# Small tiles in pools of their own: a decoder layer whose matmul pages are moved within SBUF

## The chip, the cores and the metric

The kernel runs on one core of a Trainium2 chip. The metric is the device time of one execution in microseconds; several executions give a median. A separate execution is taken with the hardware profiler, and all rows below are from that one.

## What is computed

One layer of a hybrid decoder, for 512 tokens of width 1024, in float32. Four sub-layers follow each other, each closed by a layer norm of (alpha x + f(x)):

```python
x = layer_norm(DN_ALPHA * x + 0.5 * swiglu_ffn(x, ffn1_wg, ffn1_wu, ffn1_wd), ln1_g, ln1_b)   # d_ff 2816
y = parallel_mixers(x, w_in, ...)          # gated DeltaNet with 8 heads beside a convolution module
x = layer_norm(DN_ALPHA * x + y, ln2_g, ln2_b)
x = layer_norm(DN_ALPHA * x + memory_cross_attention(x, mem, w_xq, w_xkv, w_xo), ln3_g, ln3_b)  # 256 memory tokens
x = layer_norm(DN_ALPHA * x + 0.5 * swiglu_ffn(x, ffn2_wg, ffn2_wu, ffn2_wd), ln4_g, ln4_b)

def swiglu_ffn(x, w_gate, w_up, w_down):
    return (silu(x @ w_gate) * (x @ w_up)) @ w_down
```

The mixers project the stream, run a short convolution and a chunked delta rule per head, gate and normalise its output, run a convolution of width 31 with a channel norm, project both branches, mix them with two gates and project again.

## The kernel before

**Split products.** A float32 matrix product is made of three products of a reduced-precision type. Each operand is split into an upper part (ScalarE's copy, line 267) and a lower part (VectorE's subtraction, line 268); upper x upper, lower x upper and upper x lower are added up in PSUM. All weights come as 253 chunks of 128 x 1024 (512 KB) from one array, `wall`, in the order of their use, and SyncE loads them ahead (line 111) into three pages `w`; the split writes to pages `wh` and `wl`.

**Two forms of product.** In the first, line 280 (`a_steps`), the weights are the stationary operand and the stream is the moving one: `xh` and `xl`, 512 tokens (256 in the first four tiles of a stage, `a_four_first`), for eight feature tiles one after the other. In the second, lines 328 to 330 (`b_mm` in `b_form`), tokens come out as rows: the moving operand is 512 columns of a weight chunk and the stationary one is a slice of 128 tokens of a page of activations (`hh`/`hl` in the feed-forwards, `yh`/`yl` in the mixers' output product, `mmh`/`mml` and `aoh`/`aol` in the attention). In a trace's row `acc<-wh,hh` the moving operand stands first and the stationary one second. Every product has a weight load of its own, so while one product's moving operand streams, the stationary operand of the next is loaded.

**Stages.** First feed-forward to 374 us (gate and up tiles, then the down product from 249 us); the mixers to 1013 us: gating and convolution tiles to 460 us, the heads' chains between the products of the input projection to 827 us, the branch projections, gates and convolution projection to 967 us (their moving pages are called `pg`, line 280), and the output product; the attention to 1198 us; the second feed-forward to the end, its down product from 1421 us. TensorE keeps the order of the program. In the heads' stage an agenda (`Agenda`, `PACE`) decides between which products each step of a head's chain stands; that order is fixed when the program is built.

**Where pages lie.** Pools are laid out in SBUF one behind the other, tiles of a pool in the order of their first use, each padded to 32 bytes. A pool mixes large pages with small tiles (statistics, per-head columns), so that every small tile shifts the pages behind it. The addresses of the built program, modulo 512 bytes:

| pages | before | after |
|---|---|---|
| weights `w`, `wh`, `wl`; stream `xh`, `xl`; constants `con` (identity for transposes) | 128 | 128 |
| both feed-forwards' `hh`, `hl` (and chunks that live there) | 224 | 128; second feed-forward 192 |
| convolution pages `c`, later `yl` | 96, 224, 352, 480 | 0, 128, 256, 384 |
| decay pages `dd`, later `oz`, `yh` | 0 | 128 |
| heads: `kT` | 192 | 128 |
| heads: `ktok`, `MT`, `bm`, `qT`, `X`, `Y`, `kb`, `vT` | 320 | 128 |
| heads: `vb`, `AT`, `z`, `t1` | 448 | 128 |
| heads: `vn`, `S` | 0 | 128 |
| attention's `qh`, `kh`, `vh`, `mmh`, `aoh`, `pth` and lower parts | 224 | 128 |
| attention's `pe` | 480 | 128 |

The pages `pg` behind the heads use the heads' slots: the first two upper parts those of `kT`, the next three those of `qT`, the last three those of `z`; the lower parts those of `vb` (three), `Y` (three) and `kb` (two).

Of the kernel before, what the change touches and what calls it, by code (L numbers as in the profile page):

```python
# [16 lines left out]
P = 128  # L17
# [10 lines left out]
PAD = CW - 1  # L28
NCHK = SEQ // P
LATE = 20000  # L30
# spacing of the steps of a head's chains along the stream of products
# [22 lines left out]
# columns of the constant array (shapes only)  # L54
# [13 lines left out]
class Agenda:  # L68
    """Chains of work that go on beside the products; a chain yields how long it is to wait."""
# [26 lines left out]
class Weights:  # L96
    """The weight chunks in the order of their use: loaded ahead, split into two float32r parts."""
# [43 lines left out]
class LayerNorm:  # L141
    """Layer norm of the residual stream by token tiles, behind a token-major product."""

    def __init__(self, kn, pool, i, res, scale, eps, dst, to_x):
        """res: DRAM rows of the residual; to_x: the result also becomes the next stream."""
        self.kn, self.pool, self.eps, self.dst, self.to_x = kn, pool, eps, dst, to_x
        self.scale = scale
        nc = kn.nc
        self.gb = pool.tile([P, 2 * D], F32, name=kn.nm("lngb"), tag="lngb", bufs=1)
        nc.sync.dma_start(self.gb, kn.a[f"ln{i}"])  # L150
        self.rows, self.stats = [], []
        for t in range(NT):
            r = pool.tile([P, D], F32, name=kn.nm("row"), tag="row", bufs=NT)
            nc.sync.dma_start(r, res[t * P:(t + 1) * P, :])
            self.rows.append(r)
            self.stats.append(pool.tile([P, 2, 6], F32, name=kn.nm("st"), tag="st", bufs=NT))
# [14 lines left out]
    def normalise(self, t):  # L171
        nc, r, gb = self.kn.nc, self.rows[t], self.gb
        mv = self.pool.tile([P, 4], F32, name=self.kn.nm("mv"), tag="mv", bufs=NT)
        nc.vector.bn_aggr(mv[:, 0:2], self.stats[t])
        nc.vector.tensor_scalar(mv[:, 2:3], mv[:, 1:2], self.eps, None, op0=ALU.add)  # L175
        nc.gpsimd.tensor_tensor(mv[:, 3:4], mv[:, 2:3], self.kn.mh[:, 0:1], op=ALU.pow)  # L176
        hs = [slice(0, 512), slice(512, D)]
        for s in hs:
            nc.vector.scalar_tensor_tensor(r[:, s], r[:, s], mv[:, 0:1], gb[:, s], op0=ALU.subtract, op1=ALU.mult)
        for i, s in enumerate(hs):  # L180
            nc.vector.scalar_tensor_tensor(r[:, s], r[:, s], mv[:, 3:4], gb[:, D + 512 * i:D + 512 * (i + 1)],
                                           op0=ALU.mult, op1=ALU.add)
            nc.sync.dma_start(self.dst[t * P:(t + 1) * P, s], r[:, s])
# [30 lines left out]
class Kern:  # L214
    def __init__(self, nc, tc, ctx, a, nchunks):
# [11 lines left out]
        self.par = cp.tile([P, NPAR], F32, name="par")  # L227
        self.ident = self.con[:, K_ID:K_ID + P]
        self.mh = cp.tile([P, 8], F32, name="mh")

    def load_consts(self):
        nc = self.nc
        self.in_order(nc.sync.dma_start(self.con, self.a["con"]))
        self.in_order(nc.sync.dma_start(self.par, self.a["par"]))
        self.zs = []
        for i in range(4):
            z = self.dr.tile([8 * (16 * SEQ + 16)], F32, name=f"zs{i}")
            self.in_order(nc.sync.dma_start(z, self.a["zero"]))
# [26 lines left out]

    def split(self, hi, lo, src):
# [6 lines left out]
    def pin(self, ins, cols):  # L273
        """TensorE keeps the order of the program; cols: what the instruction costs."""
# [13 lines left out]
    def a_steps(self, ps, w, xh, xl, lo, hi, nk=KT):  # L288
        """ps[feature, lo:hi] = w^T x over nk tiles, one tile per step; xh(k, lo, hi), xl(k, lo, hi) give the moving parts."""
# [24 lines left out]
    def a_four_first(self, between):  # L314
        """Four tiles, the last 256 tokens of each after the first 256 of all; between[i] comes in tile i's first part."""
# [46 lines left out]
    def ffn(self, i, first, res, dst, to_x):  # L362
        nc, tc = self.nc, self.tc
        with self.psum_pool(f"psf{i}", gp=4), tc.tile_pool(name=f"ffn{i}", bufs=1, reuse_waits="tile") as pool:
# [27 lines left out]
            ln = LayerNorm(self, pool, 1 if i == 1 else 4, res, 2 * ALPHA, 4 * LN_EPS, dst, to_x)  # L392
# [5 lines left out]
    def gating(self, mp, ab):  # L398
        """ab: PSUM [16 of 128 rows, 512 tokens]: a then bt. Makes beta, exp of sums, and the decay pages."""
# [9 lines left out]
        def new(s):  # L409
            return mp.tile(sh, F32, name=self.nm(s), tag=s, bufs=1)  # L410
# [16 lines left out]
        ea = mp.tile([P, HEADS], F32, name="ea", tag="ea", bufs=1)  # L427
# [5 lines left out]
        self.gh, self.gl = (mp.tile(sh, F32R, name=n, tag=n, bufs=1) for n in ("gh", "gl"))  # L433
# [10 lines left out]
    def decay(self, mp, h):  # L444
        """exp of the decay sums, [j, (chunk, i)], zero where i < j."""
# [13 lines left out]
    def conv4(self, ps, dst, mt):  # L459
        """Causal 4-tap convolution of one feature tile, then SiLU."""  # L460
# [18 lines left out]
    def sumsq(self, hp, out, x):  # L479
        """Sums of squares of a head's rows: x [token, (chunk, feature)]."""  # L480
# [4 lines left out]
    def scaled(self, hp, tag, bufs, src, s):  # L485
        """Rows of each chunk times a column: s(c)."""
# [50 lines left out]
    def invert_blocks(self, hp, st):  # L537
        """Inverses of the 16 x 16 unit lower triangular blocks by substitution, a block to a partition."""
# [32 lines left out]
    def invert_rest(self, hp, st):  # L571
        """From 16-blocks to the whole 128 x 128 inverse: X = inverse, Y = its transpose."""
# [20 lines left out]
        # 64-blocks from 32-blocks: their lower left in X where it is used again, its transpose in Y  # L593
# [47 lines left out]
    def head_q(self, hp, h, ps, st):  # L641
# [6 lines left out]
        sq = hp.tile([P, NCHK], F32, name=self.nm("ssq"), tag="ssq", bufs=4)  # L648
# [24 lines left out]
    def scan(self, mp, hp, h, st, ozs):  # L673
# [4 lines left out]
        sso = hp.tile([P, NCHK], F32, name=self.nm("sso"), tag="sso", bufs=2)  # L678
# [42 lines left out]
    def glu(self, mp, m, pl, pg):  # L721
        """c = lin * sigmoid(gate), with PAD zeros before the first token."""
        nc = self.nc
        c = mp.tile([P, PAD + SEQ], F32, name=self.nm("c"), tag="c", bufs=8)
        self.pool_pin(nc.gpsimd.memset(c[:, 0:PAD], 0.0))
        nc.scalar.activation(c[:, PAD:], pg, AF.Sigmoid)
        nc.vector.tensor_tensor(c[:, PAD:], c[:, PAD:], pl, op=ALU.mult)
# [12 lines left out]
    def conv_norm(self, mp, cs, t):  # L740
        """LayerNorm over the channels of the convolution, then SiLU, in place in cs[:, 0:512]: one token tile."""
# [3 lines left out]
        st = mp.tile([P, 2, 6], F32, name=self.nm("st"), tag="st", bufs=2)  # L745
        mv = mp.tile([P, 4], F32, name=self.nm("mv"), tag="mv", bufs=2)
# [23 lines left out]
    def mixers(self, res, dst):  # L770
        nc, tc = self.nc, self.tc
        S = 512
        with tc.tile_pool(name="mix", bufs=1, reuse_waits="tile") as mp, ExitStack() as ctx:
            ctx.enter_context(self.psum_pool("psm", **BANKS))
            cs = []
# [17 lines left out]
            with tc.tile_pool(name="heads", bufs=1, reuse_waits="tile") as hp:  # L793
# [23 lines left out]
                def tile_job(done):  # L817
                    """The product of one weight tile, in four steps."""
# [60 lines left out]
            with self.psum_pool("psl", gp=4), tc.tile_pool(name="ln2", bufs=1, reuse_waits="tile") as lp:  # L879
                ln = LayerNorm(self, lp, 2, res, ALPHA, LN_EPS, dst, True)  # L880
# [4 lines left out]
    def xattn(self, res, dst):  # L885
        nc, tc = self.nc, self.tc
        N = NMEM
        with self.psum_pool("psx", gp=4), tc.tile_pool(name="xat", bufs=1, reuse_waits="tile") as xp:
# [34 lines left out]
            def scores(hd):  # L923
                """Softmax of one head's scores, token-major."""
                pes[hd] = []
                for t in range(NT):
# [7 lines left out]
                    sm = xp.tile([P, 4], F32, name=self.nm("sm"), tag="sm", bufs=8)  # L934
# [45 lines left out]
            ln = LayerNorm(self, xp, 3, res, ALPHA, LN_EPS, dst, True)  # L980
# [116 lines left out]
```

## Time and profile before

| | before |
|---|---|
| median of 3 runs | 1556.01 us (1554.59 to 1556.44) |
| span of the profiled execution | 1553.0 us |
| TensorE busy, products | 1521.6 us, 7826 |
| VectorE, ScalarE, GpSimd busy | 859.2, 554.4, 198.1 us |
| moved by DMA | 166.70 MB, 107 GB/s over the span |

A product is shown busy from its start to a modelled end, and the next one starts before that end; busy TensorE therefore tells nothing of its rate. The rate is read from the starts. A row of the timeline gives the start, the duration, the engine, the line and the operands; rows of one kind that overlap are merged ("x2").

### The profile page before, as it was taken

The page shows a single profiled execution, that of the slowest core. Times are in us where ns is not written, and L with a number is a line of the kernel's source. Part 1 is how long each engine was busy: PE and PEld are TensorE (multiplying, and loading weights), DVE is VectorE, ACT ScalarE, POOL GpSimd, SP SyncE. Part 2 cuts the span into 40 slices and gives each one's busy share as a digit, 9 for nine tenths or more (in the row PEclk, how much of TensorE's full clock was granted, in tenths as well). Part 3 has the DMA queues.
Part 4 walks back from the last instruction along what each step waited for, and adds up shares of the span by engine and source line. Part 5 has one row for each costly group of instructions (what it writes and reads, how often), then busy time and mean ns, then how long its engine had stood idle before and what let it go on. Part 6 is the DMA issues. An engine that isn't in the chain of part 4 may idle for free.

```text
span 1553.0 us, 19809 instructions
## 1 busy us (share of the span) xinstructions
PE 1521.6 (98%) x7826; PEld 1266.5 (82%) x7826; DVE 859.2 (55%) x1240; ACT 554.4 (36%) x1035; POOL 198.1 (13%) x320
## 2 busy tenths in 40 slices
PE   8999999999999999999999999999999999999998
PEld 6888888888867787888888888899889888888886
DVE  4333332228799999999735525565756333333235
ACT  5222222123343554556554523144523232222110
POOL 0000000001034535565400000000000000000000
PEclk9999999999999999999999999999999999999999
DMA  8323333335122332222222232474324432233231
GB/s 319 101 96 99 97 102 95 95 92 180 46 67 74 103 91 78 78 78 78 80 96 81 82 97 95 175 247 149 120 82 163 135 95 95 95 96 96 94 95 54
DMA packets 62812, 166.70 MB, mean 107 GB/s; under 512 B 18624, under 2 KB 18752, under 8 KB 62144
## 3 DMA queue, kind: packets, MB, share of 16 engines
q1 hardware_dynamic: 62720, 165.44, 32.7%
q8 instruction: 61, 1.00, 0.3%
q14 instruction: 31, 0.25, 0.0%
HBM read 154.41 MB, written 12.06 MB: 107 GB/s over the span
## 4 chain that ended last, share of the span: by engine, by line
PE 83%; DVE 9%; issue 3%; POOL 2%; DMA 1%; ACT 1%; SPq 0%; DVEq 0%; POOLq 0%; ACTq 0%
PE acc L280 54%; PE acc L328 4%; PE gp L328 4%; PE acc L329 4%; PE gp L330 4%; PE acc L330 4%; PE gp L329 4%; DVE a L737 4%; PE inv L280 1%; DVE wl L268 1%; POOL rk L474 1%; DVE ug L450 1%; DVE qT L466 1%; DMA w<-wall 1%; PE gp L191 1%
## 5 line engine op out<-in xcount | busy, mean ns | idle before, releaser
L268 DVE TENSOR_TENSOR wl<-w,wh 128x1024 fp32r<-128x1024 f32 (+1 forms) x260 | 309.6, 1195 | 427.8 <-ACT wh L267 427.3
L280 PE MATMUL acc<-xh,wh 128*128 128x512 f32 (+1 forms) x1384 | 533.4, 386 | 6.1 <-ACT wh L267 4.9
L280 PE MATMUL acc<-xh,wl 128*128 128x512 f32 (+1 forms) x1384 | 519.7, 376 | 0.1
L280 PE MATMUL acc<-xl,wh 128*128 128x512 f32 (+1 forms) x1384 | 519.3, 376 | 0.0
L267 ACT CAST wh<-w 128x1024 fp32r<-128x1024 f32 (+1 forms) x260 | 265.6, 1026 | 451.3 <-PE acc L280 219.7
L280 PEld LDWEIGHTS acc<-xh,wh 128*128 128x128 f32 x1384 | 261.1, 189 | 49.4 <-ACT wh L267 4.9
L280 PEld LDWEIGHTS acc<-xl,wh 128*128 128x128 f32 x1384 | 260.4, 188 | 48.4 <-DVE xl L268 0.5
L280 PEld LDWEIGHTS acc<-xh,wl 128*128 128x128 f32 x1384 | 261.3, 189 | 42.6 <-DVE wl L268 1.0
L737 DVE SCALAR_TENSOR_TENSOR a<-c,par,a 128x512 f32<-128x512 f32 x232 | 175.3, 788 | 0.2
L176 POOL TENSOR_TENSOR mv<-mv,mh 128x1 f32<-128x1 f32 x16 | 15.5, 970 | 1043.8 <-DVE mv L175 917.0
L383 DVE TENSOR_TENSOR s<-s,acc 128x512 f32<-128x512 f32 x44 | 30.2, 687 | 113.2 <-PE acc L280 113.1
L382 ACT ACTIVATE s<-acc 128x512 f32<-128x512 f32 x44 | 26.3, 597 | 163.6 <-PE acc L280 163.6
L280 PE MATMUL acc<-pg,wh 128*128 128x512 f32 x256 | 81.3, 395 | 0.0
L328 PE MATMUL gp<-wh,hh 128*128 128x512 f32 x176 | 69.9, 397 | 0.0
L328 PE MATMUL acc<-wh,hh 128*128 128x512 f32 x176 | 69.8, 396 | 0.0
L330 PE MATMUL gp<-wh,hl 128*128 128x512 f32 x176 | 69.8, 396 | 0.0
L329 PE MATMUL gp<-wl,hh 128*128 128x512 f32 x176 | 69.8, 396 | 0.0
L330 PE MATMUL acc<-wh,hl 128*128 128x512 f32 x176 | 69.8, 396 | 0.0
L329 PE MATMUL acc<-wl,hh 128*128 128x512 f32 x176 | 69.8, 396 | 0.0
L280 PEld LDWEIGHTS acc<-pg,wh 128*128 128x128 f32 x256 | 48.0, 188 | 11.0 <-DVE pg L268 0.2
L474 POOL TENSOR_TENSOR xb<-xb,xt 32x14 f32<-32x14 f32 (+6 forms) x112 | 54.0, 482 | 8.8
L280 PE MATMUL acc<-pg,wl 128*128 128x512 f32 x128 | 50.4, 394 | 0.0
(280 smaller groups left out, 1830.9 us busy)
## 6 DMA issues: line engine op xcount, KB each, us to landing
w<-wall SPq DMA_DIRECT2D x252, 512.0 KB
res<-row SPq DMA_DIRECT2D x24, 256.0 KB
row<-res SPq DMA_DIRECT2D x12, 512.0 KB
lngb<-ln SPq DMA_DIRECT2D x4, 1024.0 KB
xs<-xT SPq DMA_DIRECT2D x8, 256.0 KB
row<-x SPq DMA_DIRECT2D x4, 512.0 KB
scm<-MT SPq DMA_DIRECT2D x8, 256.0 KB
X<-zs SPq DMA_DIRECT2D x8, 256.0 KB
```

The lines of the kernel that those rows point to most:

```text
L191: kn.nc.tensor.transpose(tp[:, c * P:(c + 1) * P], r[:, k * P:(k + 1) * P], kn.ident)
L267: self.nc.scalar.copy(hi, src)
L268: self.nc.vector.tensor_tensor(lo, src, hi.bitcast(F32), op=ALU.subtract)
L280: self.pin(self.nc.tensor.matmul(out, **kw), out.shape[-1] * (1 if kw["lhsT"].dtype == F32R else 4))
L328: mm(ps, lhsT=th, rhs=wh, start=first, stop=False)
L329: mm(ps, lhsT=th, rhs=wl, start=False, stop=False)
L330: mm(ps, lhsT=tl, rhs=wh, start=False, stop=last)
L382: nc.scalar.activation(s, g, AF.Silu)
L383: nc.vector.tensor_tensor(s, s, u, op=ALU.mult)
L450: eng.tensor_tensor(ug, bc(self.con[:, K_U:K_U + P].unsqueeze(1), [P, NCHK, P]), bc(g[:, :, h:h + 1].bitcast(F32), [P, NCHK, P]), op=ALU.mult)
L474: self.pool_pin(self.nc.gpsimd.tensor_tensor(out, x, y, op=op))
L737: nc.vector.scalar_tensor_tensor(a, c[:, j:j + SEQ], w(j), a, op0=ALU.mult, op1=ALU.add)
```

## The change

Small tiles (statistics of the norms, per-head columns, gating vectors) go to a second pool beside each stage's pool, which lies behind the large pages (`pages`, `small`). The parameter page is padded to 512 columns, and the constant -1/2 for GpSimd's powers (`mh`) moves into its spare columns. The convolution's pages get 544 columns in place of 542. In the second feed-forward a tile of 16 columns (64 bytes), which nothing uses, is put ahead of the pages. Comments are dropped and lines shift. The instructions of every engine stand in the same order with the same operations and shapes; they differ in addresses, in the operand of GpSimd's powers (`par` for `mh`), and two waits of SyncE's loads (`ms`, and the last `lngb`) name another product of TensorE, 12 products later and 2 earlier.

```diff
+CPAGE = 544
 class LayerNorm:
-    def __init__(self, kn, pool, i, res, scale, eps, dst, to_x):
+    def __init__(self, kn, pool, small, i, res, scale, eps, dst, to_x):
...
-            self.stats.append(pool.tile([P, 2, 6], F32, name=kn.nm("st"), tag="st", bufs=NT))
+            self.stats.append(small.tile([P, 2, 6], F32, name=kn.nm("st"), tag="st", bufs=NT))
...
-        mv = self.pool.tile([P, 4], F32, name=self.kn.nm("mv"), tag="mv", bufs=NT)
+        mv = self.small.tile([P, 4], F32, name=self.kn.nm("mv"), tag="mv", bufs=NT)
...
-        self.par = cp.tile([P, NPAR], F32, name="par")
+        self.par = cp.tile([P, 512], F32, name="par")
         self.ident = self.con[:, K_ID:K_ID + P]
-        self.mh = cp.tile([P, 8], F32, name="mh")
+        self.mh = self.par[:, NPAR:NPAR + 8]
...
-        self.in_order(nc.sync.dma_start(self.par, self.a["par"]))
+        self.in_order(nc.sync.dma_start(self.par[:, 0:NPAR], self.a["par"]))
...
+    @contextmanager
+    def pages(self, name):
+        with self.tc.tile_pool(name=name, bufs=1, reuse_waits="tile") as big, \
+                self.tc.tile_pool(name=name + "s", bufs=1, reuse_waits="tile") as small:
+            yield big, small
...
     def ffn(self, i, first, res, dst, to_x):
-        with self.psum_pool(f"psf{i}", gp=4), tc.tile_pool(name=f"ffn{i}", bufs=1, reuse_waits="tile") as pool:
+        with self.psum_pool(f"psf{i}", gp=4), self.pages(f"ffn{i}") as (pool, small):
+            if not first:
+                pool.tile([P, 16], F32, name="shift")
...
     def gating(self, mp, ab):
         def new(s):
-            return mp.tile(sh, F32, name=self.nm(s), tag=s, bufs=1)
+            return self.small.tile(sh, F32, name=self.nm(s), tag=s, bufs=1)
...
-        sm = lambda s, bufs=4: hp.tile([P, NCHK], F32, name=self.nm(s), tag=s, bufs=bufs)
+        sm = lambda s, bufs=4: self.small2.tile([P, NCHK], F32, name=self.nm(s), tag=s, bufs=bufs)
...
-        c = mp.tile([P, PAD + SEQ], F32, name=self.nm("c"), tag="c", bufs=8)
+        c = mp.tile([P, CPAGE], F32, name=self.nm("c"), tag="c", bufs=8)
...
-        with tc.tile_pool(name="mix", bufs=1, reuse_waits="tile") as mp, ExitStack() as ctx:
+        with self.pages("mix") as (mp, self.small), ExitStack() as ctx:
             ctx.enter_context(self.psum_pool("psm", **BANKS))
+            self.small.tile([P, 8], F32, name="pad")
...
-            with tc.tile_pool(name="heads", bufs=1, reuse_waits="tile") as hp:
+            with self.pages("heads") as (hp, self.small2):
...
-        with self.psum_pool("psx", gp=4), tc.tile_pool(name="xat", bufs=1, reuse_waits="tile") as xp:
+        with self.psum_pool("psx", gp=4), self.pages("xat") as (xp, small):
```

## Rows read from the trace of the kernel before

**Rows 1.** The page's first part: busy us, share of the span, instructions.

```profile
PE 1521.6 (98%) x7826; PEld 1266.5 (82%) x7826; DVE 859.2 (55%) x1240; ACT 554.4 (36%) x1035; POOL 198.1 (13%) x320
```

**Rows 2.** Busy us of each engine in stretches; granted clock, DMA share, GB/s last.

```profile
249.00:374.00 125.00, 125.00 (x544) 100.75 (x543) 49.93 (x65) 29.80 (x35) 2.97 (x3) 1.00 0.34 110
...
460.00:827.00 367.00, 354.91 (x2260) 295.47 (x2259) 311.19 (x486) 193.52 (x531) 164.34 (x282) 1.00 0.27 85
...
967.00:1013.00 46.00, 46.00 (x208) 37.41 (x207) 28.75 (x44) 10.82 (x13) 2.90 (x3) 1.00 0.43 159
1013.00:1198.00 185.00, 184.54 (x1137) 164.44 (x1136) 115.05 (x205) 73.31 (x124) 4.85 (x5) 1.00 0.47 157
```

**Rows 3.** Timeline of TensorE, first feed-forward's gate and up tiles: start us, us.

```profile
19.71 0.39 PE L280 MATMUL acc<-xh,wh 128*128 128x512 f32 x1
...
25.83 0.39 PE L280 MATMUL acc<-xh,wh 128*128 128x512 f32 x1
```

**Rows 4.** The same view, first feed-forward's down product.

```profile
299.71 0.39 PE L329 MATMUL acc<-wl,hh 128*128 128x512 f32 x1
...
302.99 0.39 PE L328 MATMUL acc<-wh,hh 128*128 128x512 f32 x1
```

**Rows 5.** The same view, attention: values' product, then output product.

```profile
1127.70 0.39 PE L962 MATMUL acc<-pth,vh 128*128 128x512 f32 x1
...
1129.08 0.39 PE L962 MATMUL acc<-pth,vh 128*128 128x512 f32 x1
...
1132.25 0.39 PE L964 MATMUL acc<-ptl,vh 128*128 128x512 f32 x1
1132.48 0.40 PE L328 MATMUL acc<-wh,aoh 128*128 128x512 f32 x1
...
1133.88 0.39 PE L328 MATMUL acc<-wh,aoh 128*128 128x512 f32 x1
```

**Rows 6.** The same view, mixers' output product.

```profile
988.86 0.39 PE L328 MATMUL gp<-wh,yh 128*128 128x512 f32 x1
...
991.65 0.39 PE L328 MATMUL gp<-wh,yh 128*128 128x512 f32 x1
```

**Rows 7.** The same view, products behind the heads.

```profile
847.22 0.39 PE L280 MATMUL acc<-pg,wh 128*128 128x512 f32 x1
...
849.77 0.62 PE L280 MATMUL acc<-pg,wh 128*128 128x512 f32 x2
...
955.65 0.39 PE L280 MATMUL acc<-pg,wl 128*128 128x512 f32 x1
...
956.57 0.62 PE L280 MATMUL acc<-pg,wh 128*128 128x512 f32 x2
```

**Rows 8.** The attention's memory pages: their loads (first and last start us).

```profile
L904 SPq DMA_DIRECT2D ms<-memT x4: 327/328/454, 1022.0 to 1038.7; - x4
```

**Rows 9.** Timeline of TensorE, products of 256 columns in three places.

```profile
376.37 0.28 PE L280 MATMUL acc<-xh,wh 128*128 128x256 f32 x1
...
379.42 0.28 PE L280 MATMUL acc<-xh,wl 128*128 128x256 f32 x1
...
1060.87 0.28 PE L280 MATMUL acc<-mmh,wh 128*128 128x256 f32 x1
...
1063.39 0.28 PE L280 MATMUL acc<-mmh,wh 128*128 128x256 f32 x1
...
1198.82 0.28 PE L280 MATMUL acc<-xh,wh 128*128 128x256 f32 x1
...
1201.46 0.28 PE L280 MATMUL acc<-xh,wl 128*128 128x256 f32 x1
```

**Rows 10.** TensorE by line and shape, heads' stage: busy us, mean ns of one.

```profile
L280 PE MATMUL prep<-kbT,kT 128*128 128x128 f32 x64 | 8.4, 275 | 0.0
L280 PE MATMUL inv<-X,bm 128*128 128x128 f32 x64 | 8.4, 274 | 0.0
```

**Rows 11.** What TensorE waited for from 374 to 827 us: us, times, longest.

```profile
PE prep L285 <- DVE kb L510: 5.1, 4, 1.7
```

More of the change, by code (lines that the diff above doesn't have):

```diff
@@ L141 @@
 class LayerNorm:
-    def __init__(self, kn, pool, i, res, scale, eps, dst, to_x):
-        self.kn, self.pool, self.eps, self.dst, self.to_x = kn, pool, eps, dst, to_x
+    def __init__(self, kn, pool, small, i, res, scale, eps, dst, to_x):
+        self.kn, self.pool, self.small, self.eps, self.dst, self.to_x = kn, pool, small, eps, dst, to_x
         self.scale = scale
@@ L391, in ffn @@
                     self.first_loads = False
-            ln = LayerNorm(self, pool, 1 if i == 1 else 4, res, 2 * ALPHA, 4 * LN_EPS, dst, to_x)
+            ln = LayerNorm(self, pool, small, 1 if i == 1 else 4, res, 2 * ALPHA, 4 * LN_EPS, dst, to_x)
             self.b_form(FT, lambda k: hh[k], lambda k: hl[k], ln, ahead=(4, pool, "hh", "hl", FT) if to_x else None)
@@ L426, in gating @@
         V.scalar_tensor_tensor(sp, p, 2.0, sp, op0=ALU.mult, op1=ALU.add)
-        ea = mp.tile([P, HEADS], F32, name="ea", tag="ea", bufs=1)
+        ea = self.small.tile([P, HEADS], F32, name="ea", tag="ea", bufs=1)
         nc.scalar.activation(ea, self.pcol(C_ALOG, 8), AF.Exp)
@@ L432, in gating @@
         V.reciprocal(self.beta, e)
-        self.gh, self.gl = (mp.tile(sh, F32R, name=n, tag=n, bufs=1) for n in ("gh", "gl"))
+        self.gh, self.gl = (self.small.tile(sh, F32R, name=n, tag=n, bufs=1) for n in ("gh", "gl"))
         self.split(self.gh, self.gl, self.g)
@@ L647, in head_q @@
         self.transpose4(tq, qT)
-        sq = hp.tile([P, NCHK], F32, name=self.nm("ssq"), tag="ssq", bufs=4)
+        sq = self.small2.tile([P, NCHK], F32, name=self.nm("ssq"), tag="ssq", bufs=4)
         self.sumsq(hp, sq, tq)
@@ L677, in scan @@
         o = st["vb"]
-        sso = hp.tile([P, NCHK], F32, name=self.nm("sso"), tag="sso", bufs=2)
+        sso = self.small2.tile([P, NCHK], F32, name=self.nm("sso"), tag="sso", bufs=2)
         for c in range(NCHK):
@@ L723, in glu @@
         nc = self.nc
-        c = mp.tile([P, PAD + SEQ], F32, name=self.nm("c"), tag="c", bufs=8)
+        c = mp.tile([P, CPAGE], F32, name=self.nm("c"), tag="c", bufs=8)
         self.pool_pin(nc.gpsimd.memset(c[:, 0:PAD], 0.0))
-        nc.scalar.activation(c[:, PAD:], pg, AF.Sigmoid)
-        nc.vector.tensor_tensor(c[:, PAD:], c[:, PAD:], pl, op=ALU.mult)
+        nc.scalar.activation(c[:, PAD:PAD + SEQ], pg, AF.Sigmoid)
+        nc.vector.tensor_tensor(c[:, PAD:PAD + SEQ], c[:, PAD:PAD + SEQ], pl, op=ALU.mult)
         return c
@@ L744, in conv_norm @@
         zn = [mp.tile([P, 512], F32, name=self.nm("zn"), tag="a31", bufs=2) for _ in range(2)]
-        st = mp.tile([P, 2, 6], F32, name=self.nm("st"), tag="st", bufs=2)
-        mv = mp.tile([P, 4], F32, name=self.nm("mv"), tag="mv", bufs=2)
+        st = self.small.tile([P, 2, 6], F32, name=self.nm("st"), tag="st", bufs=2)
+        mv = self.small.tile([P, 4], F32, name=self.nm("mv"), tag="mv", bufs=2)
         tps = []
@@ L878, in mixers @@
             ctx.close()
-            with self.psum_pool("psl", gp=4), tc.tile_pool(name="ln2", bufs=1, reuse_waits="tile") as lp:
-                ln = LayerNorm(self, lp, 2, res, ALPHA, LN_EPS, dst, True)
+            with self.psum_pool("psl", gp=4), self.pages("ln2") as (lp, small):
+                ln = LayerNorm(self, lp, small, 2, res, ALPHA, LN_EPS, dst, True)
                 self.b_form(KT, lambda k: yh[k], lambda k: yl[k], ln)
@@ L933, in scores @@
                         mm(sp[:, 0:N], lhsT=ql[k][:, ts], rhs=kh[:, k], start=False, stop=(kk == 1))
-                    sm = xp.tile([P, 4], F32, name=self.nm("sm"), tag="sm", bufs=8)
+                    sm = small.tile([P, 4], F32, name=self.nm("sm"), tag="sm", bufs=8)
                     nc.vector.tensor_reduce(sm[:, 0:1], sp[:, 0:N], axis=AX.X, op=ALU.max)
@@ L979, in xattn @@
                     values(hd - 2, pts[hd - 2])
-            ln = LayerNorm(self, xp, 3, res, ALPHA, LN_EPS, dst, True)
+            ln = LayerNorm(self, xp, small, 3, res, ALPHA, LN_EPS, dst, True)
             self.b_form(KT, lambda k: oh[k], lambda k: ol[k], ln, ahead=(2, xp, "mmh", "mml", 4))
```

## The prediction

> **What bounds the kernel now.** I read the stages first [rows 1, 2]. [...] So the time is a count of products times the time from one product's start to the next one's, which I call the pitch. A busy share of 98% does not say that this pitch is as short as it can be. I then took the pitch out of timelines, as the start of the last row minus that of the first, over the number of steps; the rows round to 10 ns, so long stretches are needed.
>
> In the first feed-forward, products of the stream against weights of 512 columns stand 6.12 us apart over 27 steps [rows 3]: 226.7 ns, with no variation. In the same feed-forward's down product, with as many columns, 14 steps take 3.28 us [rows 4]: 234.3 ns. In the first, weights and stream both lie at 128 modulo 512; in the second the streamed chunk lies at 128 and the stationary page at 224. That could come from the form of the product. Three things speak for the addresses.
> First, in the attention [rows 5] the values product streams a page of 224 against stationary pages of 224: 14 steps from 1129.08 to 1132.25 us are 226.4 ns each. Then the output product begins, with streamed chunks at 128 and stationary pages at 224, and its six steps to 1133.88 are 233.3 ns. Both have contiguous moving pages of 512 columns and a slice of 128 columns as weights; one has equal residues, the other not.
> Second, the mixers' output product [rows 6] has the form of the down product, but its stationary pages lie at 0 and, every third time, at 96, 224, 352 or 480; its 12 steps take 2.79 us, 232.5 ns, another figure in the same form.
> Third, behind the heads pages at 192, 320 and 448 stream against weights at 128: 11 steps take 2.55 us [rows 7], 231.8 ns; where the streamed page is one at 192 in three of four steps (the first two pages of a tile), 0.92 us over 4 steps gives 230 ns.
> I conclude that the weight load for the next product and the stream of the present one hinder each other unless their addresses agree modulo 512, and that the price is 3 to 8 ns a product of 512 columns.
>
> **The change, part by part.** It moves no instruction: on all engines the same operations stand in the same order. Two of SyncE's waits name another product of TensorE. The load of the memory page waits for one 12 products later (some 2.8 us at 232 ns), but that one lies in the mixers' output product, over by 1013 us [rows 2], and the load is issued at 1022.0 us [rows 8]: nothing is late. The other waits for two products fewer. The exponent constant now lies behind the parameters in their page; the same GpSimd operation reads as many bytes. Both cost nothing.
>
> What remains is products times the fall of their pitch:
> 1. First feed-forward, down product: 22 feature tiles x 2 halves x 4 token tiles x 3 = 528 products, from 234.3 to 226.7, as all its pages go to 128: 528 x 7.6 = 4.0 us.
> 2. Attention: the values' projection (8 x 2 x 2 x 3 = 96) and the output product (8 x 2 x 4 x 3 = 192), both from unequal to equal residues: 288 x 7.6 = 2.2 us.
> 3. Second feed-forward, down product: 528 again, but from 224 to 192, with the chunks still at 128. No row shows weights 64 bytes above the stream. Bounds: 226.7 (equal addresses) and 234.3 (as now). The nearest row is the one with the two exchanged, stream at 192 and weights at 128, 230 ns [rows 7]; I take 230.5, since its neighbours give 231.8: 528 x 3.8 = 2.0 us, with 0 and 4.0 as ends.
> 4. Products behind the heads, 16 tiles x 24 = 384, with pages now at 128: from about 231 to 226.7, but TensorE's transposes interrupt the first half, and after an interruption the pitch needs some products to settle (the six steps from 1127.70 to 1129.08 are 230 ns each [rows 5]), so I take 227.2: 384 x 3.8 = 1.5 us, 0.7 if it settles seldom.
> 5. Mixers' output product, 192: the upper-part pages go to 128, but the lower parts use the slots of the convolution's pages, which are 2176 bytes long and so lie at 0, 128, 256 and 384. Of three products two then load weights at 128, and the third does so in two of eight feature tiles. The ends are 226.7 and the present 232.5; I take 229.5: 192 x 3 = 0.6 us, from 0 to 1.1.
> 6. A loss: products of 256 columns that open the next stage with weights in the feed-forward's or the attention's pages (224 against a stream at 128) stand 3.05 us apart over 26 steps [rows 9], 117.3 ns, while those with both at 128 take 0.12 us each (1198.82 to 1201.46, 22 steps, 120.0 ns). There are 192 behind the first feed-forward and 96 before the second: 288 x 2.7 = 0.8 us lost. The keys' projection (stream 224, weights 128) is 2.52 us over 21 steps [rows 9], 120.0 ns already: nothing.
> 7. The heads' stage: its products against weights of 512 columns have equal residues already. Its float32 products of 128 columns change from 192, 320 and 448 to 128. Those that already have both operands at 320 (X against bm) take 274 ns as modelled, those 128 bytes apart (kbT against kT) 275 [rows 10]: nothing to gain or lose in sight. TensorE's own waits there are small: the longest in total is 5.1 us, on a VectorE step [rows 11]. I take 0. There are 296 such products of two passes each and 160 transposes, some 750 passes; 2 ns each either way, twice what lies between the two groups of rows 10, is 1.5 us up or down.
> The other engines' work changes in its addresses only, and outside the heads they wait for TensorE (VectorE 50 of 125 us in the first down product), so a few ns more or less of theirs stay hidden. TensorE, 3% quicker there, asks for weights at some 114 instead of 110 GB/s, while the attention stage moves 157 GB/s [rows 2] without a wait that shows: transfers stay hidden too.
> Sum: 4.0 + 2.2 + 2.0 + 1.5 + 0.6 - 0.8 = 9.5 us. It is made on a profiled execution of 1553.0 us; the runs have a median of 1556.01, 3 us more that lie around the span and do not change. 1556.0 - 9.5 = 1546.5 us, 0.6% less.
>
> [...] The pitch is 226.7 ns in one stretch and 234.3 in another at the same clock and the same columns [rows 3, 4]. [...]
>
> **The rivals.**
> A. The form decides, not the address: a product that streams weight chunks stays at 234.3, one that streams pages at 231. Then only the 256-column rows could move, and the time is 1556 us. For it: nearly all slow rows are of those forms, and all of the kernel's pitch of 226.7 in long stretches has the other form. Against it: rows 5 and the change of pitch with the page in rows 6. Chance 0.08. [...]
> B. The heads get slower. With identity, weights and pages all at 128, each float32 pass could collide where now pages lie apart. Place: the heads' stage; price: the 750 passes of item 7; at 12.7 ns a pass it takes all of the gain, from 17 ns on the kernel is slower by 3.2 us, 1559.2 us. Against it: the pair that has equal residues now costs 274 ns like the others [rows 10]. Chance 0.04.
> C. The second feed-forward goes to an end: 226.7 gives 2.0 us more, 1544.5; 234.3 gives 1548.5. Both are in the forecast's range and share its 0.88.
>
> **How the numbers follow.** Forecast 0.88, A 0.08, B 0.04. Best ends together: 9.5 + 2.0 (item 3) + 0.5 (item 5) + 1.5 (item 7) = 13.5, 1542.5 us. Worst: 9.5 - 2.0 - 0.8 - 0.6 - 1.5 = 4.6, 1551.4. The medians themselves may be off by about 1 us; the ends all coming together is unlikely, so I widen only the fast end: 1541.5 to 1551.5. That leaves out A, B and little else. A change of 0.2%, 3.1 us, is about what a measurement can tell from none: faster 0.88, same 0.08, slower 0.04.
>
> **What would show it.** Right: timelines of the first down product and the attention's output product with starts 226.7 ns apart; those behind the heads settling to it within some ten products after each transpose; the second feed-forward's down product between 226.7 and 234, my figure being 230.5; the 256-column opening products at 120 ns; stages before 249 us and from 1210 to 1421 us as before. Wrong: a down product of the first feed-forward that still takes 234 ns (rival A), a longer heads' stage with more ns for its float32 passes (B), or TensorE waiting for weights in a down product.

## The result, and the profile after

The changed kernel takes 1546.49 us (median of 4 runs, 1545.63 to 1546.70), the kernel before in the same comparison 1556.22 us (1554.59 to 1556.44): a ratio of 0.9937, 95% interval 0.9923 to 0.9951, or 9.7 us less. The forecast was 1546.5 us. The profiled execution spans 1544.5 us where that of before spans 1553.0 [rows 1].

The page of the changed kernel, sections 1 and 5 (the latter: instruction group, count, busy us, mean ns of one, idle before):

```profile
span 1544.5 us, 19809 instructions
...
PE 1513.6 (98%) x7826; PEld 1266.5 (82%) x7826; DVE 858.9 (56%) x1240; ACT 554.9 (36%) x1035; POOL 197.8 (13%) x320
...
L288 PE MATMUL acc<-pg,wh 128*128 128x512 f32 x256 | 80.4, 391 | 0.0
L336 PE MATMUL gp<-wh,hh 128*128 128x512 f32 x176 | 69.2, 393 | 0.0
```

There are as many instructions as before, TensorE's share is the same 98%, and it is busy 8 us less. The share tells nothing of the gain; the pitch, the time from one start to the next, does. Lines have moved: 280 is now 288, and 328 to 330 are 336 to 338. What follows are stretches of TensorE's timeline in the changed kernel (start us, length us, engine, line, operation, count), each shown by its first and its last row.

The first feed-forward's down product (20 steps), which answers to [rows 4]:

```profile
297.31 0.39 PE L336 MATMUL acc<-wh,hh 128*128 128x512 f32 x1
...
301.85 0.39 PE L338 MATMUL acc<-wh,hl 128*128 128x512 f32 x1
```

4.54 us over 20 steps are 227.0 ns (226.7 from the starts in ns), where 234.3 stood. Next the attention's output product (17 steps, as the last rows of [rows 5]) and the products behind the heads (15 steps, as [rows 7]; a row with x2 counts two products):

```profile
842.74 0.62 PE L288 MATMUL acc<-pg,wh 128*128 128x512 f32 x2
...
846.14 0.62 PE L288 MATMUL acc<-pg,wh 128*128 128x512 f32 x2
...
1131.01 0.39 PE L336 MATMUL acc<-wh,aoh 128*128 128x512 f32 x1
...
1134.86 0.39 PE L338 MATMUL acc<-wh,aol 128*128 128x512 f32 x1
```

3.40 us over 15 steps are 226.7 ns, 3.85 over 17 are 226.5. The mixers' output product, as [rows 6], keeps a mixture. Here are three products of wh with yh; between the first two rows the lower part yl lies at 384 modulo 512, between the last two at 256, while the chunks stream from 128:

```profile
980.18 0.39 PE L336 MATMUL acc<-wh,yh 128*128 128x512 f32 x1
...
980.86 0.39 PE L336 MATMUL acc<-wh,yh 128*128 128x512 f32 x1
...
981.56 0.39 PE L336 MATMUL acc<-wh,yh 128*128 128x512 f32 x1
```

Three products take 0.68 us with yl 256 bytes from the stream and 0.70 us (0.693 in ns) with yl 128 bytes from it. And the second feed-forward's down product, 15 steps with pages at 192 and chunks at 128:

```profile
1497.28 0.39 PE L338 MATMUL gp<-wh,hl 128*128 128x512 f32 x1
...
1500.78 0.40 PE L338 MATMUL gp<-wh,hl 128*128 128x512 f32 x1
```

3.50 us over 15 steps: 233.3 ns, where the forecast had 230.5. The opening products of 256 columns, as the first of [rows 9], 10 steps behind the first feed-forward:

```profile
376.73 0.28 PE L288 MATMUL acc<-xh,wl 128*128 128x256 f32 x1
...
377.93 0.28 PE L288 MATMUL acc<-xl,wh 128*128 128x256 f32 x1
```

1.20 us over 10 steps: 120.0 ns, up from 117.3, as forecast. In e2 below, these products stand between the two.

A table by parts says where the time went. A part lasts from the start of its first product to that of the next part's first product, which is the same product in both kernels:

| part (products) | before, us | after, us | difference | forecast |
|---|---|---|---|---|
| first feed-forward, down (528) | 125.44 | 121.48 | -3.96 | -4.0 |
| attention: values, output | 46.20 + 46.72 | 45.48 + 45.34 | -2.10 | -2.2 |
| second feed-forward, down (528) | 123.46 | 122.97 | -0.49 | -2.0 |
| behind the heads (384) | 51.98 + 44.33 | 51.30 + 43.52 | -1.48 | -1.5 |
| mixers' output (192) | 46.43 | 45.74 | -0.69 | -0.6 |
| openings of three stages, 256 columns | 74.25 | 75.08 | +0.84 | +0.8 |
| heads' stage | 427.73 | 427.70 | -0.03 | 0 |
| all others | | | -0.04 | 0 |
| first feed-forward, first half, and what lies ahead of it | 248.87 | 248.35 | -0.52 | 0 |

The last line is no work of the change: it differs from execution to execution (243.0 to 244.3 us from the first product on, among the kernels below in which nothing of it was changed). Without it the parts give -7.95 us.

### The profile page after: what moved, and what is told of

It is laid out like the page before. It is cut to its first block, busy times and chain, and to the rows that moved or that the text cites. A ratio compares the mean times of both kernels' runs of the same rounds, so it can differ in the third digit from the quotient of the medians.

```text
span 1544.5 us, 19809 instructions
## 1 busy us (share of the span) xinstructions
PE 1513.6 (98%) x7826; PEld 1266.5 (82%) x7826; DVE 858.9 (56%) x1240; ACT 554.9 (36%) x1035; POOL 197.8 (13%) x320
## 4 chain that ended last, share of the span: by engine, by line
PE 82%; DVE 10%; issue 4%; POOL 3%; DMA 1%; ACT 1%; SPq 0%; DVEq 0%; POOLq 0%; ACTq 0%
PE acc L288 54%; PE acc L336 4%; PE acc L338 4%; PE acc L337 4%; PE gp L338 4%; PE gp L337 4%; PE gp L336 4%; DVE a L747 4%; PE inv L288 1%; DVE wl L276 1%; POOL rk L484 1%; DVE ug L460 1%; DVE qT L476 1%; DMA w<-wall 1%; PE scan L288 1%
## 5 line engine op out<-in xcount | busy, mean ns | idle before, releaser
L177 POOL TENSOR_TENSOR mv<-mv,par 128x1 f32<-128x1 f32 x16 | 15.5, 969 | 1035.6 <-DVE mv L176 910.2
```

## The experiments

All kernels below compute the whole reference. I call **distance** the address of a stationary page less that of the stream, modulo 512. The theory to be tested is that a product pays for a distance other than 0 between its stream and the page loaded for the next product; the rivals are that the form decides, or the stage.

**e1: the second feed-forward at distance 0.**

```diff
-            if not first:
-                pool.tile([P, 16], F32, name="shift")
```

> The second feed-forward's pages lie at 128 instead of 192, as far from the streamed chunks (128) as those of the first feed-forward are: not at all. Theory of the address distance: the 528 products of its down product go from the 233.3 ns that they have in the changed kernel to 226.7 ns, 528 x 6.6 = 3.5 us, so about 1543.0 us, 0.9915 of the time before. Rival, that something in the second feed-forward's own stage or in the form of its product holds the pitch: it stays at 233, and the time at 1546.5 us (0.9937).

Measured: 1542.21 us (1541.88 to 1543.47, 5 runs), ratio to before 0.9921 (0.9909 to 0.9934). The same down product, 18 steps:

```profile
1496.69 0.39 PE L336 MATMUL gp<-wh,hh 128*128 128x512 f32 x1
...
1500.77 0.39 PE L336 MATMUL gp<-wh,hh 128*128 128x512 f32 x1
```

4.08 us over 18 steps: 226.7 ns; the part takes 119.45 us in place of 122.97, 3.52 less. Sixty-four bytes at one place are worth that; the stage and the form are not what held it.

**e2: one part undone.** The first feed-forward's pages back at 224.

```diff
             if not first:
                 pool.tile([P, 16], F32, name="shift")
+            else:
+                pool.tile([P, 24], F32, name="shift")
```

> One part of the change undone: the first feed-forward's pages go back to 224, by an unused tile of 96 bytes ahead of them; all else is as in the changed kernel. Theory of the address distance: its 528 down products go from 226.7 back to 234.3 ns (+4.0 us), and the 192 products of 256 columns behind it from 120.0 back to 117.3 ns (-0.5 us): 1550.0 us, 0.9960 of the time before. Rival (the gain of that stage came from the separate pool of small tiles or from waits, not from the residue): it stays at 1546.5 us, with 226.7 ns.

Measured: 1550.12 us (1549.59 to 1552.01, 7 runs), ratio 0.9971 (0.9960 to 0.9981). Its down product, 16 steps:

```profile
298.75 0.39 PE L337 MATMUL acc<-wl,hh 128*128 128x512 f32 x1
...
302.50 0.40 PE L338 MATMUL acc<-wh,hl 128*128 128x512 f32 x1
```

3.75 us over 16 steps: 234.4 ns. The part takes 125.44 us again, to the hundredth what it took before, with the separate pool of small tiles in place. So the residue made that gain, and nothing else of the change did. The second half of the expectation missed: the 256-column products behind it, expected back at 117.3 ns and worth 0.5 us, stand 118.5 ns apart over the 26 steps of [rows 9], and the part that they open takes 24.77 us where it took 24.99 in the changed kernel and 24.53 before. Only half of what the change cost there comes back with the address.

**e3: distance 256.**

```diff
-                pool.tile([P, 16], F32, name="shift")
+                pool.tile([P, 64], F32, name="shift")
```

> The second feed-forward's pages lie at 384 modulo 512, 256 bytes from the streamed chunks at 128. Theory that only equal residues modulo 512 are free of the loss: the pitch in its down product is anywhere above 229 ns, likely 230 to 234.3, and the time 1545 to 1547 us (0.993 to 0.994). Theory that the period is 256 bytes, formed from the mixers' output product of the changed kernel, where pages 256 bytes off show 226.9 ns: 226.7 ns as at 128, and 1543.0 us (0.9915).

Measured: 1544.34 us (1542.94 to 1545.03, 5 runs), ratio 0.9932 (0.9920 to 0.9945), between the two expectations. The down product decides; its 18 steps stand as in e1:

```profile
1496.66 0.39 PE L336 MATMUL gp<-wh,hh 128*128 128x512 f32 x1
...
1500.74 0.39 PE L336 MATMUL gp<-wh,hh 128*128 128x512 f32 x1
```

226.7 ns, and 119.45 us for the part. A distance of 256 costs nothing, so equality modulo 512 is not what counts. What e3 is longer than e1, 2.0 us by the spans, lies in the heads, whose code and addresses are the same in both. A table of four windows of its profile (busy us of each engine, granted clock, DMA share, GB/s):

```profile
510.00:520.00 10.00, 9.31 (x55) 7.84 (x53) 10.00 (x14) 4.72 (x7) 1.73 (x1) 1.00 0.22 79
520.00:521.40 1.40, 0.21 (x8) 0.21 (x10) 1.40 (x3) 0.00 (x0) 0.00 (x0) 1.00 0.18 17
521.40:524.90 3.50, 3.50 (x23) 2.81 (x20) 3.50 (x6) 2.28 (x4) 2.32 (x4) 0.52 0.05 7
525.00:530.00 5.00, 5.00 (x50) 3.89 (x49) 3.73 (x6) 3.48 (x14) 4.29 (x10) 1.00 0.33 105
```

TensorE has waited 1.9 us for VectorE, does 32x32 products, and then runs at a granted clock of 0.52 for 3.5 us. Products of 512 columns stand 0.43 us apart there, and the execution loses 1.5 us; the rest lies mainly near 594 us, where the execution of e1 gained 0.6 us on those of e3 and of the changed kernel. The profiled executions of the changed kernel and of e1 went through the same place at 1.00.

**e4: the distance made from the other side.** The stream xh, xl goes to 224, the chunks stay at 128, in every projection from the activations.

```diff
+        cp.tile([P, 24], F32, name="push")
         self.xh = cp.tile([P, NT, KT, P], F32R, name="xh")
         self.xl = cp.tile([P, NT, KT, P], F32R, name="xl")
+        cp.tile([P, 104], F32, name="back")
```

> The undoing of equality from the other side: the activations xh and xl, which stand still in the long projections, lie at 224 modulo 512, and the weights' chunks, which stream there, stay at 128. That is a distance of 96 bytes in some 1,900 products of 512 columns and 256-column ones beside them, all of which had 226.7 ns before and after the change. Theory of the address distance: the products of the feed-forwards' first halves go from 226.7 to 234.3 ns; 1,920 of them give 14.6 us, and with those in the heads' stage, partly hidden, 16 to 25 us: 1562 to 1571 us, 1.005 to 1.010 of the time before. Rival, that this form of product, with the activations standing still, is fast whatever its addresses: 1546.5 us, 226.7 ns.

The expectation has the roles exchanged: in these products xh and xl stream and the chunks stand still (`lhsT=wh, rhs=xh`). The distance is 128 - 224 = -96, which is 416. Measured: 1564.43 us (1563.87 to 1565.23, 4 runs), ratio 1.0053 (1.0038 to 1.0069): slower than the kernel before. The second feed-forward's first half, 18 steps:

```profile
1299.65 0.39 PE L290 MATMUL acc<-xh,wl 128*128 128x512 f32 x1
...
1303.86 0.39 PE L290 MATMUL acc<-xh,wl 128*128 128x512 f32 x1
```

4.21 us over 18 steps: 233.9 ns, 233.3 in the mean of all of them. This form, which had 226.7 ns in both kernels [rows 3], loses it with its addresses. The first halves grew by 7.9 and 6.4 us, the heads' stage, where part is hidden, by 1.9. Rival A, the form, is out from both sides.

**e5: the heads' pages mixed again.**

```diff
-            with self.pages("heads") as (hp, self.small2):
+            with tc.tile_pool(name="heads", bufs=1, reuse_waits="tile") as hp:
+                self.small2 = hp
```

> The heads' small tiles go back among the heads' large pages, so that those pages lie at several residues again, also behind the heads; all else is as in the changed kernel. Theory of the address distance: the products behind the heads, 226.9 ns in the changed kernel, go to about 230 where their page is neither 0 nor 256 bytes from the chunks, some 0.5 to 1.5 us; the heads' own stage, 453.0 us in both kernels, doesn't move by more than 0.5 us: 1547 to 1548 us, 0.9942 of the time before. Rival (the float32 products of the heads lose by having all their pages at 128, and the gain behind them hides it): the heads' stage gets shorter by 1 us or more, and the time is 1546 us or less.

Measured: 1548.30 us (1547.23 to 1550.19, 5 runs), ratio 0.9951 (0.9939 to 0.9963). The products behind the heads take 51.79 + 43.95 us, 0.92 more than in the changed kernel. The heads' stage was 1.87 us longer in the profiled execution. Of that, 0.5 and 1.5 us were lost at about 491 and 522 us, where seven and eight products stand 0.43 us apart, as in e3 (from 520 to 526 us the mean granted clock is 0.72); the rest of the stage differs by less than 0.2 us. It didn't get shorter, so rival B's hidden cost isn't there.

**e6: all at distance 0 or 256.** e1, and the convolution's pages 2304 bytes long, so that yl lies at 128 or 384.

```diff
-CPAGE = 544
+CPAGE = 576
...
-            if not first:
-                pool.tile([P, 16], F32, name="shift")
```

> The second feed-forward's pages at 128, and the convolution's pages 2304 bytes long instead of 2176, so that the mixers' output product has its lower parts at 128 or 384 only, 0 or 256 bytes from the chunks. Theory of a period of 256 bytes: the second feed-forward gives 3.5 us, and the products of the mixers' output product that still stand at 232 to 234 ns (some 60 to 80 of 192) fall to 227, another 0.4 us: 1542.6 us, 0.9913 of the time before, 44.3 us in place of 44.8 in that stage. Theory of a period of 512: the pages at 384 cost what those at 0 and 256 cost now, and that stage stays at 44.8 us or above; 1543.0 us.

Measured: 1542.47 us (1542.08 to 1544.62, 5 runs), ratio 0.9927 (0.9913 to 0.9940); no difference from e1 that the runs can tell. The profile can: the mixers' output product takes 45.32 us in place of 45.74, all of it at 226.7 ns. The span of 1540.3 us is the shortest of all kernels here.

**e7, e8, e9: a scan.** In the second feed-forward the pages of every two feature tiles get a distance of their own. In the first half of the down product 24 products in a row have the same.

```diff
-            if not first:
-                pool.tile([P, 16], F32, name="shift")
+            cur = P
+            steps = [0, 4, 16, 32, 64, 96, 128, 160, 192, 224, 240]
...
+                        off = (P + steps[f // 2] - cur) % 512
+                        t = pool.tile([P, SEQ + off // 4], F32R, name=self.nm(part), tag=f"{part}{f}", bufs=1)
+                        pair.append(t[:, off // 4:off // 4 + SEQ])
```

> A scan: in the second feed-forward each pair of stationary pages has a distance of its own from the streamed chunks, 0, 4, 16, 32, 64, 96, 128, 160, 192, 224 and 240 bytes. In the first half of the down product 24 products in a row have one distance. Theory of a period of 256 bytes with a free place only near 0: 226.7 ns at 0, 233.3 at 64, 234.3 at 96, 232.5 at 128, between 230 and 234 at the rest; the loss is even about 128, so that 160 is as 96 and 192 as 64. What happens at 4 and 16 bytes is open: if the beginning within a line of 32 or 64 bytes doesn't matter, 226.7; if only equality counts, 230 or more. Rival of the form: all the same. The mean of the half is then near 232 ns, and the time some 2.5 us above that of all pages at 128: 1545 us.

> The scan's other half: 256, 260, 288, 320, 352, 384, 416, 448, 480, 496 and 508 bytes. Theory of a period of 256 bytes: the pitch at 256 + x is that at x in the first half of the scan, 226.7 ns at 256, 233.3 at 320, 234.3 at 352, 232.5 at 384. Theory of a loss that depends on which of the two addresses is ahead (a distance taken modulo 512 alone): the values at 256 + x and at x differ, except at 256 itself, where 226.7 was measured in a kernel with all pages there. Time about 1545 us.

> A finer scan of the same kind, on the side where the stationary page lies a little below a multiple of 256 bytes from the stream. Distances modulo 256, in this order: 8, 24, 200, 208, 216, 228, 232, 236, 244, 248, 252 (every second page is 256 bytes on). The scans before had 226.7 ns at 0, 240 and 252, 233.3 at 16, 32 and 224, 232.5 at 4 and 228.9 at 192. Theory of a free stretch that begins between 224 and 240 and ends at 0: 226.7 at 244, 248 and 252, the border somewhere among 228, 232 and 236, 232 to 234 at 8 and 24, 229 to 233 at 200 to 216. Rival (only single distances are free, 240 and 252 among them by chance): 230 or more at some of 244 and 248.

One execution each, 1549.32, 1548.28 and 1547.13 us; the whole is no measure here, since the granted clock differs: 0.995, 0.997 and 0.998 in the mean, where the changed kernel's profiled execution has 0.999 (e7's heads' stage took 3.3 us more than the changed kernel's). Rows of e7, each 24 products behind the one above it, with distances of 160, 192, 224 and 240 between them:

```profile
1455.97 0.39 PE L338 MATMUL acc<-wh,hl 128*128 128x512 f32 x1
...
1461.57 0.40 PE L338 MATMUL acc<-wh,hl 128*128 128x512 f32 x1
...
1467.08 0.39 PE L338 MATMUL acc<-wh,hl 128*128 128x512 f32 x1
...
1472.67 0.39 PE L338 MATMUL acc<-wh,hl 128*128 128x512 f32 x1
...
1478.12 0.39 PE L338 MATMUL acc<-wh,hl 128*128 128x512 f32 x1
```

5.60, 5.51, 5.59 and 5.45 us for 24 products. In e9, distances of 244, 248 and 252:

```profile
1459.66 0.39 PE L338 MATMUL acc<-wh,hl 128*128 128x512 f32 x1
...
1465.26 0.39 PE L338 MATMUL acc<-wh,hl 128*128 128x512 f32 x1
...
1470.85 0.39 PE L338 MATMUL acc<-wh,hl 128*128 128x512 f32 x1
...
1476.29 0.40 PE L338 MATMUL acc<-wh,hl 128*128 128x512 f32 x1
```

5.60, 5.59 and 5.44 us. The pitch of the last 12 of each 24, from the starts in ns:

| distance modulo 256 | pitch, ns |
|---|---|
| 0, 240, 252 | 226.7 |
| 192 | 228.9 |
| 8, 200, 228, 232 | 230.5 to 231.1 |
| 24 | 231.1, then 230.0 |
| 208, 216, 236 | 231.7 to 232.0 |
| 4 | 232.4 |
| 16, 32, 64, 128, 160, 224, 244, 248 | 233.3 |
| 96 | 234.2 |

The eight values that e8 repeats 256 bytes on are those of e7 to a tenth of a nanosecond (4, 32, 64, 96, 128, 160, 192, 224): the period is 256 bytes at all distances that were tried twice. The loss isn't even about 128, as I had expected: a page 64 bytes above the stream gives 233.3, one 64 bytes below it (192) 228.9. Nor is there a free stretch below 0: 240 and 252 are free, 244 and 248 cost 233.3, so the rival of e9's expectation holds, single distances. And the pitch is not a function of the distance alone: with 24 the first half of the down product settled at 231.1 and the second at 230.0, over the same pages.

**e10: one load in three at a distance.** hh at 128, hl 64 bytes above (the scan's code with `steps = {"hh": 0, "hl": 64}`).

> In the second feed-forward the pages of upper parts (hh) lie at 128 like the chunks, those of lower parts (hl) 64 bytes above, so that one weight load in three is at a distance. With all three at 64 bytes the pitch was 233.3 ns, with none 226.7. Theory of one price for each load at a distance: (233.3 + 2 x 226.7) / 3 = 228.9 ns on the mean, the loss in the product that runs while hl is loaded. Rival, formed from the mixers' output product of the changed kernel, where such a load is followed by 232.4 and then 234 ns: two slow products for one load, about 231 ns on the mean, 528 x 4.4 = 2.3 us above all pages at 128.

Measured: 1544.78 us in one execution; the down product takes 121.79 us, 2.34 above e1. Three products and the start of a fourth:

```profile
1442.25 0.39 PE L336 MATMUL acc<-wh,hh 128*128 128x512 f32 x1
1442.48 0.39 PE L337 MATMUL acc<-wl,hh 128*128 128x512 f32 x1
1442.71 0.40 PE L338 MATMUL acc<-wh,hl 128*128 128x512 f32 x1
1442.95 0.39 PE L336 MATMUL acc<-wh,hh 128*128 128x512 f32 x1
```

Over the whole product the three pitches are 228.3, 229.2 and 235.8 ns, mean 231.1. One page at a distance costs 13.3 ns in three products, where three such pages cost 3 x 6.6 = 20. And the slow product is that of hl itself, not the one that runs while hl is loaded. That speaks against the mechanism that I had in mind, so I made one more.

**e11: every load at distance 0 from the stream of the product just before it.** e10, with the chunk wl 64 bytes above wh, and the pages laid out modulo 256.

```diff
+                if not i and not j:
+                    kn.wp.tile([P, 16], F32, name="push")
                 pl = pool.tile([P, page], F32R, name=f"wl{i}_{j}", tag=tl, bufs=bufs)
...
+        cp.tile([P, 112], F32, name="back")
         self.xh = cp.tile([P, NT, KT, P], F32R, name="xh")
```

> Which distance counts: from the running product's stream to the page that is loaded meanwhile for the next product, or to the page that the running product has loaded for itself? In the second feed-forward the lower parts hl stay 64 bytes above the upper parts hh as in the kernel with one load in three at a distance, and now the chunk wl, which streams just while hl is loaded, lies 64 bytes above wh too (everywhere in the kernel). So each page there is loaded under a stream 0 or 256 bytes from it, while two of three products stream at 64 bytes from their own page. Theory that the stream and the load of the next page hinder each other: 226.7 ns in that down product, 119.5 us for it. Rival, that a product's own page and stream count: the product of hl stays at 236, that of wl gets slow too, and the mean is 231 or more. Elsewhere one load in three is now 64 bytes from the stream (448 in the first feed-forward's down product), which by the kernel before costs 4.4 ns a product: the first halves of the feed-forwards go to 231 ns, and the whole to 1550 to 1556 us.

Measured: 1561.17 us in one execution; the second feed-forward's down product takes 121.80 us, as in e10.

```profile
1463.50 0.40 PE L339 MATMUL acc<-wh,hh 128*128 128x512 f32 x1
1463.73 0.39 PE L340 MATMUL acc<-wl,hh 128*128 128x512 f32 x1
1463.96 0.39 PE L341 MATMUL acc<-wh,hl 128*128 128x512 f32 x1
1464.19 0.40 PE L339 MATMUL acc<-wh,hh 128*128 128x512 f32 x1
```

Its pitches are 232.5, 231.7 and 229.2 ns, mean 231.1. My theory asked for 226.7 and falls in that form. The rival, a product's own page and stream, has the mean right, but it had the product of hl at 236, and that one is now the fastest. What both kernels share is that some of the pages or chunks lie 64 bytes off the rest.

e11 has an assumption of its own: that a load meets only the stream of the product just before it. The load of hl in these rows:

```profile
1463.73 0.19 PEld L341 LDWEIGHTS acc<-wh,hl 128*128 128x128 f32 x1
```

It begins with the row of that product (wl, hh), but the row of the one before (wh, hh: 1463.50 + 0.40) has 0.17 us to run, and its stream lies 64 bytes from hl. Ends of products are modelled, so the trace does not tell whether that stream is still being read. If it is, e11's loads were not all free of a distance.

The whole is 5 us over the expectation's upper end: besides the first halves (4.8 and 4.2 us above e1) and the first down product (2.8 us), which I had counted, the smaller parts of 512-column products grew too, by 0.4 to 0.9 us each, while those of 256 columns (the attention's opening and keys) got 0.4 us shorter each.

## Why the prediction was right, and where it wasn't

**The reading of the pitch, and the addresses as its cause: right.** e1, e2 and e4 move one residue each and move the pitch with it, in three places and in both directions, by 3.5, 4.0 and 18 us. The price is 6.6 to 7.6 ns a product of 512 columns; the runs don't show what in TensorE takes that time.

A rival that the prediction doesn't name, that TensorE meets the traffic of other engines or of DMA at these addresses, can be settled from the trace of before. Of 497 steps in a row of its first down product, 216 have neither VectorE nor ScalarE nor GpSimd at work and take 234.3 ns on the mean; 221, in which at least one of them works all the time, take 234.4. And in the second, a stretch without DMA (its share, next to last, is 0.00):

```profile
1515.00:1520.00 5.00, 5.00 (x23) 4.04 (x22) 1.22 (x1) 1.05 (x1) 0.00 (x0) 1.00 0.00 0
```

The steps in it take 234.3 ns as well. The loss needs none of that traffic.

**Items 1, 2, 4, 5 and 6: right in size**, each within 0.1 us (see the table), and 1, 2 and 4 in their cause, the address. Item 5 was right for a partly wrong reason: I had let a lower part at 384 cost as much as one at 0 or 256, and it costs nothing, while one at 0 or 256 takes 13 ns (0.680 and 0.693 us for three products). The mean came out at 228.9 ns, where I had 229.5. Item 6 took the whole rise of the 256-column products for the address; e2, with the address of before behind the first feed-forward, got back only half of it (0.22 of 0.46 us), so what makes the other half stays open.

**Item 7, the heads: right.** 427.73 and 427.70 us, and X against bm takes 275 ns where 274 stood.

**Item 3, the second feed-forward: the term that was mis-sized.** I had 230.5 ns and 2.0 us; it is 233.3 ns and 0.49 us, though within the ends that I gave. The step that failed is taking the row "with the two exchanged", stream 64 bytes above the page, for its mirror image. (That row's 230 ns is 229.0 from the starts in ns.) The scan shows both: a page 64 bytes below the stream 228.9 ns, one 64 bytes above it 233.3. So the 192 of this change costs 3.5 us against 128.

**Modulo 512: wrong.** The period is 256, by e3 and by e8 beside e7. In this change only the mixers' output product has pages at 256 from the stream, so the sum didn't feel it.

**The mechanism, the next page's load against the running stream: not shown.** It gave the right answer wherever all pages of a product move together, which nearly all of the change does. e11 takes the two apart, and the plain form, load against the stream of the one product before it, falls there: 231.1 ns where it asked for 226.7. A load that also meets the stream of the product before that is not excluded.

**The median: right to the hundredth by luck.** The sum was 9.5 us, the parts gave 8.0 and the spans 8.5; the medians fell by 9.7. I had put the 3 us between the span of before and its median around the span, as something fixed. In the runs made beside e1 the time around the span is 1.8 us each time. So the median of before lies 1.4 us above its profiled execution (1553.0 + 1.8 = 1554.8), that of the changed kernel 0.2 above its own (1544.5 + 1.8 = 1546.3). The spans of before vary with the granted clock: in the later comparisons 1551.7 to 1553.3 us at a mean of 0.998 or 0.999, 1555.6 at 0.995; all four runs of the changed kernel had 0.999. So a lower clock in the executions behind the median of before is likely, but their clocks are not on record. A sum too large by 1.5 us and a median that fell by 1.8 us more than the parts stood against each other. By the parts alone it would have been 1556.0 - 8.0 = 1548.0 us, close to rival C's slow end, 1548.5.

## What to carry to other kernels

When TensorE is busy 98% of the time, measure the pitch in long stretches of each kind of product, and compare them: two figures for the same shape at the same clock (here 226.7 and 234.3 ns, both at 1.00) are a loss that no busy share shows. For products like these, of 512 columns with a weight load each, give all pages and chunks that TensorE reads the same address modulo 256 bytes (226.7 ns in e1 and e3). One odd page among three cost two thirds of what three cost (e10: 13.3 of 20 ns), and a distance need not be cheap because its opposite is (228.9 ns at 192, 233.3 at 64). Here that took 12 us off without moving an instruction: 1542.21 us against 1554.45 side by side, with the second feed-forward at 128 too.

## What was not expected of the hardware

- 226.7 ns a product of 512 columns is reached at single distances (0, 240, 252 modulo 256) and kept exactly; all other distances of the scan lie between 228.9 and 234.2 ns. The starts in ns show repeating patterns (at 64 in the changed kernel 231 and 236 by turns; at 96 in the kernel before 237, 238, 230, 235, 235, 233, 232), and the pitch that a stretch settles into is not fixed by the distance (24: 231.1 in one half, 230.0 in the other); whether what ran before it decides is not shown.
- Products of 256 columns can go the other way: 117.3 ns at a distance of 96 in the kernel before, 118.5 at the same distance in e2, 120.0 at 0; e4's, at 416, are no quicker than 120. Where a page serves both kinds, the 512-column ones decide: 7.6 against 2.7 ns.
- After 1.9 us of waiting inside the heads the granted clock fell to 0.52 for 3.5 us in the execution of e3 and to 0.72 in the mean of 6 us in that of e5; it stayed at 1.00 there in the changed kernel's, where TensorE had waited as long (1.9 us), and in e1's. The fall at about 522 us cost 1.5 us in e3 and 1.5 in e5. It hides differences of this size in medians; a table by parts, from the start of one product to that of another, shows them.
- Open: what in TensorE takes the time. e11 excludes a load that meets only the stream of the product just before it (231.1 ns where that asks for 226.7); no run here tells what takes its place.
